# A two-layer trunk on one core: where the operands of the paired products are formed, and how many accumulators a pair unit has

## The chip, the cores and the metric

The kernel runs on one core of one Trainium2 chip. The metric is the device time of one launch in microseconds (us). TensorE (PE) multiplies, VectorE (DVE), ScalarE (ACT) and GpSimd (POOL) do elementwise work, and SyncE (SP), ACT and POOL issue transfers (DMA). Each engine works through its own queue in order and waits on semaphores for the others.

## The reference, cut to what matters

Two layers over 640 frames: 512 of a new stream and 8 x 16 of running streams, with 1024 channels. The first layer mixes by spatial gating and a gated convolution, the second by attention; after each mixer comes the same ConvFFN, and the change touches only that:

```python
def _conv_ffn(x, prev, w_up, conv_w, w_down):
    z, st = _causal_dwconv(x @ w_up, conv_w, prev)   # 1024 -> 2 * 2816, width 3
    gate, up = jnp.split(z, 2, axis=-1)
    return (jax.nn.silu(gate) * up) @ w_down, st     # 2816 -> 1024
```

`x` is RMS-normed before it enters; the outputs are the residual streams and the new states.

## The kernel before

**Precision.** A product in full precision is three PE passes: each operand is split into a high part (a cast by ACT, `hi`) and a low part (operand minus high part, by DVE, `lo`), and PE adds high x high, high x low and low x high. `part` (L133) does such a split; the program's names end in h and l (`hh`/`hl`, `sh`/`sl`, `whi`/`wlo`, `fbh`/`fbl`). `added` (L99) makes the low part another way: ACT writes minus the high part, and a transfer issued by POOL adds the source on top.

**Layout.** Channels lie on the 128 partitions, frames along the free side, in two halves of HT = 320. The 1024 input channels are 8 chunks `h[0..7]`, walked in the order `KORD` = 0, 2, 4, 6, 1, 3, 5, 7.

**The up-projection, 22 steps j for each layer, each with a gate block and an up block of 128 outputs.** Steps 0 to 3 are *full units*: 48 matmuls a block (8 chunks x 3 passes x 2 halves), and `pad_evac` (L329) multiplies the sums by `rb`, the inverse norm of each frame, on their way out of PSUM. Steps 4 to 21 are *pair units*: gate and up, the even and odd channel chunks and the two halves of the frames form a 2 x 2 product that is computed with seven products instead of eight (a Strassen-Winograd scheme). A product is 12 matmuls of 128 x 320 (four pairs of chunks x 3 passes). Their operands must be normed beforehand:

- `forms(p, ...)` (L145), for each of the four pairs p of chunks: DVE writes the normed chunks `y` (two operations over 640 frames), then their sums T1 to T4 (six operations over 320), T1 over a part of `y`, T2 to T4 into a `raw` buffer. The latter become `fbh`, `fbl` by `added`, with a transfer that reads the `raw` buffer. It is called after step 0 (p = 0, 1) and after step 1 (p = 2, 3), behind that step's convolution and gating (`act`, L489).
- `settle(p, h, form)` (L162): splits the eight `y` back into the tiles `hh`, `hl` of the chunks. These are the tiles that the full units read, so a chunk can be settled only when the last full unit has read it. The loop runs over p, so over the chunks 0, 1, 2, ... in the code.
- `pair_weights` (L171) loads a gate and an up block into two `raw` buffers, adds and subtracts in place on DVE (L180), and splits the seven weight operands. There are four `raw` buffers in all; full units, forms, pair units and down blocks share them.

**PSUM** has eight banks: two tiles `zx` of two banks, one tile `d` of two (down blocks and every third full unit), two tiles `aux` of one. A pair unit held two accumulators in the two halves of one `zx` tile, Z (the product y2a) and X (y1a, then T2, T1 and y2b added on), and a third, Y (T3, then T4), in an `aux` tile. Between the products `snap` (ACT, tiles `sn`) copies what has been summed so far: p1 after y1a, p7 after T3, u after T2; DVE makes the outputs `zg`, `zu` (tiles `zp`) of them.

**Down blocks.** Each pair unit carries two blocks of the down-projection of the part before it, each 24 matmuls into `d`, passed as `downs` and put between the products so that a snap has time. Their weights come by `weights_down` (L112): a load by SP, a cast by ACT (L120), its negative (L121), and a transfer by POOL (L122) that completes `wlo`.

**Order.** The code gives dependences and priorities; a scheduler settles the order on every engine when the program is built. Matmuls of different products, and of neighbouring units, are thus interleaved.

Of the kernel before, what the change touches and what calls it, by code (L numbers as in the profile page):

```python
# [8 lines left out]
F32 = mybir.dt.float32  # L9
# [3 lines left out]
ALU = mybir.AluOpType  # L13
# [3 lines left out]
P = 128  # L17
# [36 lines left out]
class Core:  # L54
# [106 lines left out]

    def settle(self, p, h, form):  # L162

        ys, fb = form
        for y, (hi, lo) in zip(ys, h):
            self.part(hi, lo, y)
        pick = lambda t, i: (t[0][:, i * HT:(i + 1) * HT], t[1][:, i * HT:(i + 1) * HT])
        return dict(y1a=pick(h[0], 0), t1=pick(h[0], 1), y2a=pick(h[1], 0), y2b=pick(h[1], 1),
                    t2=pick(fb, 0), t3=pick(fb, 1), t4=pick(fb, 2))

# [31 lines left out]

    def pair_blocks(self, w, f, zg, zu, states, downs):

        nc = self.nc
        zx = self.pz.tile([P, 1024], F32, tag="zx", name=self.nm("zx"))
        Z, X = zx[:, C0:512], zx[:, 512:512 + HT]
        Y = self.aux()[:, 0:HT]
        n = TP - HT
# [7 lines left out]
        for z, st in zip((zg, zu), states):  # L217
            nc.gpsimd.tensor_copy(out=str_(z)[:, :, 0:2], in_=st.rearrange("p (s c) -> p s c", c=2))
        self.product(X, w["x11"], f, "y1a", True)
        p1 = snap(X, 1.0)  # L220
        self.product(Z, w["x12"], f, "y2a", True)
        nc.vector.tensor_tensor(out=zg[:, 2:2 + HT], in0=Z, in1=p1, op=ALU.add)
        self.product(Y, w["s3"], f, "t3", True)
        p7 = snap(Y, -1.0)
        self.product(X, w["s2"], f, "t2", False)
        u = snap(X, -1.0)
        if downs:
            downs.pop(0)()
        self.product(X, w["s1"], f, "t1", False)
        nc.vector.tensor_tensor(out=zu[:, 2 + HT:514], in0=p7[:, 0:n], in1=X[:, 0:n], op=ALU.subtract)  # L230
        nc.vector.tensor_tensor(out=str_(zu)[:, :, 2:18], in0=v(p7), in1=v(X), op=ALU.subtract)
        self.product(Y, w["x22"], f, "t4", False)
        nc.vector.tensor_tensor(out=zu[:, 2:2 + HT], in0=u, in1=Y, op=ALU.subtract)
        if downs:
            downs.pop(0)()
# [248 lines left out]
    def ffn(self, l, x, h, g, rb, ring, fb, finish, out=None):  # L484
# [40 lines left out]
        for n, (a, b) in enumerate(PARTS):  # L525
# [4 lines left out]
            for j in range(a, b):  # L530
# [3 lines left out]
                if j < NSTD:  # L534
                    w = ahead.pop(0)
                    ps = self.blocks(w, hk, first) if j == 0 else [self.blocks([v], hk)[0] for v in w]
                    if j + 2 < NSTD:
                        ahead.append(full(j + 2))
                    elif j + 2 == NSTD:
                        ahead.append(part(j + 2))  # L540
                    else:
                        dn = downs(n, acts, 0)
                        f = [self.settle(p, (h[2 * p], h[2 * p + 1]), forms[p]) for p in range(4)]
                    for z, p_, st in zip((zg, zu), ps, sts):
                        self.pad_evac(z, p_[:, C0:C0 + T], rb, st)
                else:
                    if j == NSTD:
                        w = ahead.pop(0)
                        left.pop(0)
                    else:  # L550
                        w = part(j)
                        dn = downs(n - 1, prev, left.pop(0))
                    self.pair_blocks(w, f, zg, zu, sts, dn)
                for i, z in enumerate((zg, zu)):
                    self.new_state(z, so[:, i, 18 * (j - a):18 * (j - a) + 18])
                acts.append(act(zg, zu, j))
                if j < 2:
                    forms += [self.forms(p, x, g, rb, ring, fb) for p in (2 * j, 2 * j + 1)]
            nc.scalar.dma_start(out=two(io["o_sf"][l], NB)[:, :, 18 * a:18 * b], in_=so[:, :, 0:18 * (b - a)])
# [539 lines left out]
```

## Time and profile before

| | us |
|---|---|
| median of 3 runs | 1504.85 (1503.73 to 1508.41) |
| the profiled execution | 1505.12, with a span of 1503.3 |
| PE busy | 1464.5 (97% of the span) |
| DVE, ACT, POOL busy | 1042.1 (69%), 734.4 (49%), 200.7 (13%) |
| the ConvFFN of the first layer, first pair unit on PE | from 271.3 |
| the ConvFFN of the second layer, first pair unit on PE | from 1104.8 |

Rows of the timeline give start, duration, engine, line, operation, output<-inputs and shapes; the bracket gives how long the engine had been idle and who ended that. A row of waits gives total, times and longest. A row of windows gives for a stretch its length, then for each engine the busy time and instruction count, the granted PE clock, the DMA share and GB/s. Matmuls overlap: each lasts about 0.31 us and the next starts 0.147 us later.

### The profile page before, as it was taken

Reading aid. Unit: us, or ns where it says so; the run is one execution under the profiler, and the core shown is the slowest. Engines: PE = TensorE matmul, PEld = TensorE weight load, DVE = VectorE, ACT = ScalarE, POOL = GpSimd, SP = SyncE. Lnnn points to the kernel's source line nnn. Section 1 sums busy time; section 2 is a strip of 40 time slices with the busy share of each in tenths; the row PEclk is TensorE's granted clock in tenths of the full one; section 3 lists DMA queues with packets and bytes.
Section 4 is the critical chain, followed back from the end, with each engine's and each line's share of the span. In section 5 each row is a group of like instructions: output and inputs, shape, how many; then the busy total and the mean of one; then the engine's idle time right before and its main releaser. Section 6 shows DMA issues by size and latency. Waiting matters only on the chain.

```text
span 1503.3 us, 26371 instructions
## 1 busy us (share of the span) xinstructions
PE 1464.5 (97%) x10576; PEld 1412.7 (94%) x10576; DVE 1042.1 (69%) x1791; ACT 734.4 (49%) x1324; POOL 200.7 (13%) x237
## 2 busy tenths in 40 slices
PE   8999999899999999999999999999979999999998
PEld 6999999899999999999989888888979999999998
DVE  6555437976777778676676767768787768767764
ACT  5422325745555555445545454535565555545541
POOL 5100121300100010033111111003211010001000
PEclk9999999999999999999999999999999999999999
DMA  7222214634444434253534343422365434334432
GB/s 272 78 71 72 71 43 94 166 96 116 113 116 113 104 101 118 77 168 105 186 124 142 106 130 110 148 82 88 66 159 141 103 100 119 101 93 115 112 87 85
DMA packets 72938, 168.84 MB, mean 112 GB/s; under 512 B 13728, under 2 KB 21840, under 8 KB 72688
## 3 DMA queue, kind: packets, MB, share of 16 engines
q1 hardware_dynamic: 48304, 133.79, 27.9%
q0 software_dynamic: 11808, 25.96, 10.5%
q10 hardware_dynamic: 12704, 7.41, 1.6%
q8 instruction: 83, 1.36, 0.4%
q14 instruction: 39, 0.32, 0.1%
HBM read 147.43 MB, written 11.54 MB: 106 GB/s over the span
## 4 chain that ended last, share of the span: by engine, by line
PE 81%; DMA 7%; DVE 5%; ACT 4%; issue 2%; SPq 0%; ACTq 0%; POOL 0%; DVEq 0%; POOLq 0%
PE mm L250 33%; PE zx L200 16%; PE pj L701 12%; PE aux L200 7%; DMA wlo<-w_dn 5%; PE pv L777 3%; PE po L250 3%; PE pt L770 1%; DVE hl L281 1%; DVE wlo L95 1%; PE mm L388 1%; DMA fbl<-raw 1%; PE pt L856 1%; PE sc L763 1%; DVE t L347 1%
## 5 line engine op out<-in xcount | busy, mean ns | idle before, releaser
L135 ACT CAST sh<-raw 128x1024 fp32r<-128x1024 f32 (+1 forms) x144 | 135.1, 941 | 157.9 <-PE zx L200 93.7
L250 PE MATMUL mm<-sh,wlo 128*128 128x320 f32 x864 | 197.9, 310 | 8.3 <-DMA wlo<-w_dn 8.3
L250 PE MATMUL mm<-sh,whi 128*128 128x320 f32 x864 | 196.3, 309 | 1.5 <-ACT whi L120 0.8
L250 PE MATMUL mm<-sl,whi 128*128 128x320 f32 x864 | 196.7, 308 | 0.0
L136 DVE TENSOR_TENSOR sl<-raw,sh 128x1024 fp32r<-128x1024 f32 (+1 forms) x144 | 155.8, 1090 | 56.4 <-ACT sh L135 56.2
L200 PE MATMUL zx<-hh,sh 128*128 128x320 f32 x576 | 179.2, 311 | 8.4 <-ACT sn L215 8.3
L200 PE MATMUL zx<-hl,sh 128*128 128x320 f32 x576 | 178.8, 311 | 0.6 <-DVE hl L136 0.6
L200 PE MATMUL zx<-hh,sl 128*128 128x320 f32 x576 | 176.1, 311 | 0.7 <-DVE sl L136 0.7
L347 DVE SCALAR_TENSOR_TENSOR t<-zp,cst,t 128x656 f32<-128x656 f32 x184 | 164.2, 898 | 15.0 <-ACT t L345 13.3
L94 ACT CAST whi<-raw 128x1024 fp32r<-128x1024 f32 (+3 forms) x96 | 85.8, 895 | 145.1 <-PE mm L250 81.6
L250 PEld LDWEIGHTS mm<-sh,wlo 128*128 128x128 f32 x864 | 143.6, 188 | 12.0 <-DMA wlo<-w_dn 8.5
L358 DVE TENSOR_TENSOR x<-mm,x 128x640 f32<-128x640 f32 x103 | 84.6, 821 | 93.3 <-PE mm L250 93.2
L250 PEld LDWEIGHTS mm<-sh,whi 128*128 128x128 f32 x864 | 143.6, 188 | 2.9 <-ACT whi L120 1.3
L250 PEld LDWEIGHTS mm<-sl,whi 128*128 128x128 f32 x864 | 144.3, 188 | 0.2 <-DVE sl L136 0.2
L701 PE MATMUL pj<-whi,hl 128*128 128x256 f32 x480 | 137.9, 287 | 2.8 <-DVE hl L281 2.8
L701 PE MATMUL pj<-wlo,hh 128*128 128x256 f32 x480 | 137.6, 287 | 0.0
L701 PE MATMUL pj<-whi,hh 128*128 128x256 f32 x480 | 137.3, 287 | 0.0
L95 DVE TENSOR_TENSOR wlo<-raw,whi 128x1024 fp32r<-128x1024 f32 (+3 forms) x96 | 107.9, 1128 | 33.9 <-ACT whi L94 33.4
L250 PE MATMUL mm<-hl,whi 128*128 128x320 f32 x512 | 116.9, 309 | 2.0 <-DVE hl L281 2.0
L200 PEld LDWEIGHTS zx<-hh,sh 128*128 128x128 f32 x576 | 109.1, 189 | 9.2 <-ACT sn L215 8.9
L250 PE MATMUL mm<-hh,whi 128*128 128x320 f32 x512 | 117.1, 310 | 0.0
L250 PE MATMUL mm<-hh,wlo 128*128 128x320 f32 x512 | 116.5, 309 | 0.0
(235 smaller groups left out, 3353.0 us busy)
## 6 DMA issues: line engine op xcount, KB each, us to landing
raw<-w_up SPq DMA_DIRECT2D x88, 512.0 KB
raw<-w_dn SPq DMA_DIRECT2D x36, 512.0 KB
wlo<-w_dn POOLq DMA_DIRECT2D x36, 512.0 KB, 5.9
raw<-w_c SPq DMA_DIRECT2D x24, 512.0 KB
raw<-w_ab SPq DMA_DIRECT2D x16, 512.0 KB
ck<-c_k SPq DMA_DIRECT2D x16, 512.0 KB
cv<-c_v SPq DMA_DIRECT2D x16, 512.0 KB
o_kv<-z ACTq DMA_DIRECT2D x8, 640.0 KB
```

Source lines behind the costliest of these rows:

```text
L94: nc.scalar.copy(out=hi[:, c], in_=raw[:, c])
L95: nc.vector.tensor_tensor(out=lo[:, c], in0=raw[:, c], in1=hi[:, c].bitcast(F32), op=ALU.subtract)
L135: nc.scalar.copy(out=hi, in_=src)
L136: nc.vector.tensor_tensor(out=lo, in0=src, in1=hi.bitcast(F32), op=ALU.subtract)
L200: nc.tensor.matmul(out, lhsT=l[:, c], rhs=r, start=start and p == 0 and i == 0, stop=p == 3 and i == 2, skip_group_check=True)
L250: nc.tensor.matmul(outs[h], lhsT=l, rhs=r[:, h * HT:(h + 1) * HT], start=start and k == 0, stop=stop and k == 2)
L281: nc.vector.scalar_tensor_tensor(out=lo, in0=x, scalar=gs, in1=hi.bitcast(F32), op0=ALU.mult, op1=ALU.subtract)
L347: nc.vector.scalar_tensor_tensor(out=cv[:, 0:CW], in0=zp[:, i:i + CW], scalar=w[:, i:i + 1], in1=cv[:, 0:CW], op0=ALU.mult, op1=ALU.add)
L358: self.nc.vector.tensor_tensor(out=x, in0=ps[:, C0:C0 + T], in1=x, op=ALU.add)
L388: nc.tensor.matmul(pvs[tb], lhsT=l[:, tb * P:(tb + 1) * P], rhs=r[:, (kc % 2) * 512:(kc % 2 + 1) * 512], start=kc == 0 and k == 0, stop=kc ...
L701: nc.tensor.matmul(out[tb], lhsT=l[:, tb * P:(tb + 1) * P], rhs=r[:, c:c + 256], start=kc == 0 and i == 0, stop=kc == 7 and i == 2)
L777: nc.tensor.matmul(ov[64 * hh:64 * hh + 64, i * P:n], lhsT=z[2][:, j, (2 * pair + hh) * 64:(2 * pair + hh) * 64 + 64], rhs=u[:, j * P:(j + ...
```

## The change

Four edits:

1. `forms` for p = 0, 1 and p = 2, 3 is called right after the eviction of the gate block and of the up block of steps 0 and 1, instead of behind those steps' convolution and gating.
2. `settle` splits all eight chunks in one call in the order `KORD`, the order in which the last full unit leaves them.
3. A pair unit takes three tiles: X one bank of a `zx` tile, Y and Z both `aux` tiles. Both `aux` tiles are then held by one unit.
4. The products of a pair unit stand in another order: T3, y1a, T4, y2a, T2, T1, y2b (before: y1a, y2a, T3, T2, T1, T4, y2b), with the first down block between T2 and T1 and the second between T1 and y2b. In the first pair unit of a layer T3 and T4 come first, and both down blocks come at the end.

```diff
-    def settle(self, p, h, form):
-        ys, fb = form
-        for y, (hi, lo) in zip(ys, h):
-            self.part(hi, lo, y)
+    def settle(self, h, forms):
+        for c in KORD:
+            hi, lo = h[c]
+            self.part(hi, lo, forms[c // 2][0][c % 2])
...
-    def pair_blocks(self, w, f, zg, zu, states, downs):
-        zx = self.pz.tile([P, 1024], F32, tag="zx", name=self.nm("zx"))
-        Z, X = zx[:, C0:512], zx[:, 512:512 + HT]
-        Y = self.aux()[:, 0:HT]
+    def pair_blocks(self, w, f, zg, zu, states, downs, first=False):
+        X = self.pz.tile([P, 1024], F32, tag="zx", name=self.nm("zx"))[:, 0:HT]
+        Y, Z = self.aux()[:, 0:HT], self.aux()[:, 0:HT]
...
+        self.product(Y, w["s3"], f, "t3", True)
+        p7 = snap(Y, -1.0)
+        if first:
+            self.product(Y, w["x22"], f, "t4", False)
         self.product(X, w["x11"], f, "y1a", True)
         p1 = snap(X, 1.0)
+        if not first:
+            self.product(Y, w["x22"], f, "t4", False)
         self.product(Z, w["x12"], f, "y2a", True)
         nc.vector.tensor_tensor(out=zg[:, 2:2 + HT], in0=Z, in1=p1, op=ALU.add)
-        self.product(Y, w["s3"], f, "t3", True)
-        p7 = snap(Y, -1.0)
         self.product(X, w["s2"], f, "t2", False)
         u = snap(X, -1.0)
-        if downs:
+        nc.vector.tensor_tensor(out=zu[:, 2:2 + HT], in0=u, in1=Y, op=ALU.subtract)
+        if downs and not first:
             downs.pop(0)()
         self.product(X, w["s1"], f, "t1", False)
         nc.vector.tensor_tensor(out=zu[:, 2 + HT:514], in0=p7[:, 0:n], in1=X[:, 0:n], op=ALU.subtract)
         nc.vector.tensor_tensor(out=str_(zu)[:, :, 2:18], in0=v(p7), in1=v(X), op=ALU.subtract)
-        self.product(Y, w["x22"], f, "t4", False)
-        nc.vector.tensor_tensor(out=zu[:, 2:2 + HT], in0=u, in1=Y, op=ALU.subtract)
-        if downs:
+        if downs and not first:
             downs.pop(0)()
         self.product(X, w["s4"], f, "y2b", False)
...
-                        f = [self.settle(p, (h[2 * p], h[2 * p + 1]), forms[p]) for p in range(4)]
-                    for z, p_, st in zip((zg, zu), ps, sts):
+                        f = self.settle(h, forms)
+                    for i, (z, p_, st) in enumerate(zip((zg, zu), ps, sts)):
                         self.pad_evac(z, p_[:, C0:C0 + T], rb, st)
+                        if j < 2:
+                            forms.append(self.forms(2 * j + i, x, g, rb, ring, fb))
...
-                    self.pair_blocks(w, f, zg, zu, sts, dn)
+                    self.pair_blocks(w, f, zg, zu, sts, dn, j == NSTD)
...
-                if j < 2:
-                    forms += [self.forms(p, x, g, rb, ring, fb) for p in (2 * j, 2 * j + 1)]
```

The changed file has three more lines, so L250 of before is L253 of after, L339 is L342, L347 is L350, L497 is L500.

**DVE at step 0 of the first layer.** `zp_88`, `zp_89`, `zp_90` are the evictions, `t_2153`, `t_2177` and the like the convolutions, `y` the normed chunks, `raw_...<-y` the sums. Before, the first `y` stands behind the evictions and the convolution of step 0 and behind the eviction of the next block:

```order
L347 SCALAR_TENSOR_TENSOR t_2153<-zp_88,cst,t_2153 128x656
L347 SCALAR_TENSOR_TENSOR t_2149<-zp_89,cst,t_2149 128x656
L347 SCALAR_TENSOR_TENSOR t_2153<-zp_88,cst,t_2153 128x656
L339 TENSOR_TENSOR zp_90<-mm_2193,rb_1974 128x512
L340 TENSOR_TENSOR zp_90<-mm_2193,rb_1974 128x8x16
L500 TENSOR_TENSOR t_2158<-t_2153,t_2149 128x512
L501 TENSOR_TENSOR t_2158<-t_2153,t_2149 128x128
L152 SCALAR_TENSOR_TENSOR y_2165<-x_74,gv,rb_1974 128x640
```

Now the four `y` of this step stand ahead of its evictions (the rows before these), and the sums right behind them:

```order
L343 TENSOR_TENSOR zp_88<-mm_2030,rb_1974 128x8x16
L342 TENSOR_TENSOR zp_89<-mm_2031,rb_1974 128x512
L343 TENSOR_TENSOR zp_89<-mm_2031,rb_1974 128x8x16
L156 TENSOR_TENSOR raw_2148<-y_2145,y_2144 128x320
L156 TENSOR_TENSOR raw_2165<-y_2162,y_2161 128x320
L157 TENSOR_TENSOR y_2144<-y_2144 128x320
L157 TENSOR_TENSOR y_2161<-y_2161 128x320
L350 SCALAR_TENSOR_TENSOR t_2177<-zp_89,cst,t_2177 128x656
```

So the first sums moved ahead of the convolution that they stood behind.

**PE at the start of the first pair unit of the first layer.** `hh_1573`, `hh_1642`, `hh_1768`, `hh_1894` are the settled even chunks, `hh_1579` the first odd one. Before, the unit began with the twelve matmuls of y1a; its last even chunk is followed at once by y2a in the same tile `zx_2652`:

```order
L200 MATMUL zx_2652<-hh_1768,sl_2460 128x320
L200 MATMUL zx_2652<-hh_1894,sh_2459 128x320
L200 MATMUL zx_2652<-hl_1895,sh_2459 128x320
L200 MATMUL zx_2652<-hh_1894,sl_2460 128x320
L200 MATMUL zx_2652<-hh_1579,sh_2459 128x320
L200 MATMUL zx_2652<-hl_1580,sh_2459 128x320
```

Now it begins with T3 on the formed sums, in `aux_2653`:

```order
L253 MATMUL mm_2552<-hh_1957,wlo_2301 128x320 x2
L200 MATMUL aux_2653<-fbh_2153,sh_2469 128x320
L200 MATMUL aux_2653<-fbl_2154,sh_2469 128x320
L200 MATMUL zx_2652<-hh_1573,sh_2459 128x320
L200 MATMUL aux_2653<-fbh_2153,sl_2470 128x320
L200 MATMUL aux_2653<-fbh_2170,sh_2469 128x320
```

T3 moved ahead of y1a; T4 and the first matmuls of a down block follow, ahead of all but one matmul of y2a.

**PE at T2 and T1 of the same unit.** Before, T4 (in `aux_2653`, with `sh_2463`) stood behind T2, and the next unit's matmuls between T4 and T1:

```order
L200 MATMUL zx_2652<-fbh_2352,sh_2475 128x320
L200 MATMUL zx_2652<-fbl_2353,sh_2475 128x320
L200 MATMUL zx_2652<-fbh_2352,sl_2476 128x320
L200 MATMUL aux_2653<-fbh_2174,sh_2463 128x320
L200 MATMUL aux_2653<-fbl_2175,sh_2463 128x320
```

Now T1 (with `sh_2469`) follows T2 with nothing in between, both in `zx_2652`:

```order
L200 MATMUL zx_2652<-fbh_2334,sh_2475 128x320
L200 MATMUL zx_2652<-fbl_2335,sh_2475 128x320
L200 MATMUL zx_2652<-fbh_2334,sl_2476 128x320
L200 MATMUL zx_2652<-hh_1573,sh_2469 128x320
L200 MATMUL zx_2652<-hl_1574,sh_2469 128x320
```

The work that stood between T2 and T1 moved ahead of T2.

More of the change, by code (lines that the diff above doesn't have):

```diff
@@ L160, in forms @@
         return ys, self.added(fb, ("fbh", "fbl"), t, t, 3 * HT, 3 * HT)
-    def settle(self, p, h, form):
-        ys, fb = form
-        for y, (hi, lo) in zip(ys, h):
-            self.part(hi, lo, y)
+    def settle(self, h, forms):
+        for c in KORD:
+            hi, lo = h[c]
+            self.part(hi, lo, forms[c // 2][0][c % 2])
         pick = lambda t, i: (t[0][:, i * HT:(i + 1) * HT], t[1][:, i * HT:(i + 1) * HT])
-        return dict(y1a=pick(h[0], 0), t1=pick(h[0], 1), y2a=pick(h[1], 0), y2b=pick(h[1], 1),
-                    t2=pick(fb, 0), t3=pick(fb, 1), t4=pick(fb, 2))
+        return [dict(y1a=pick(h[2 * p], 0), t1=pick(h[2 * p], 1), y2a=pick(h[2 * p + 1], 0), y2b=pick(h[2 * p + 1], 1),
+                     t2=pick(fb, 0), t3=pick(fb, 1), t4=pick(fb, 2)) for p, (_, fb) in enumerate(forms)]
     def pair_weights(self, gate, up):
```

## The prediction, on record before the result

> **What bounds the kernel now.** I read the page first, then PE's waits, then stretches of the span, then the places with waits row by row.
>
> ```profile
> span 1503.3 us, 26371 instructions
> PE 1464.5 (97%) x10576; PEld 1412.7 (94%) x10576; DVE 1042.1 (69%) x1791; ACT 734.4 (49%) x1324; POOL 200.7 (13%) x237
> PE zx L200 <- ACT sn L215: 8.3, 2, 4.6
> PE mm L250 <- DMA wlo<-w_dn: 8.3, 11, 1.6
> ```
>
> PE is the bound; nothing makes this kernel faster that doesn't take PE's idle or slow time away, 39 us at most as idle (1503.3 less 1464.5). The largest waits of the pair units are two for a snap, one in each layer, in the first pair unit. The windows around it, from the last full unit's end to the first matmul of y2b, and the steady pair units behind:
>
> ```profile
> 227.60:271.10 43.50, 43.50 (x298) 43.50 (x298) 34.77 (x60) 23.56 (x35) 8.33 (x14) 1.00 0.45 99
> 271.10:298.72 27.62, 22.03 (x126) 20.40 (x124) 26.33 (x40) 22.29 (x33) 10.47 (x6) 0.88 0.70 176
> 300.00:640.00 340.00, 336.75 (x2290) 335.27 (x2289) 248.32 (x358) 175.75 (x292) 30.26 (x49) 1.00 0.43 106
> 1063.10:1104.70 41.60, 41.60 (x286) 41.60 (x285) 35.29 (x61) 22.07 (x34) 6.42 (x10) 1.00 0.44 96
> 1104.70:1134.32 29.62, 21.38 (x124) 19.62 (x123) 26.17 (x39) 21.98 (x33) 3.54 (x6) 0.88 0.68 173
> 1145.00:1480.00 335.00, 330.55 (x2245) 328.88 (x2244) 242.10 (x348) 171.65 (x283) 27.90 (x47) 1.00 0.41 103
> 303.86 3.52 PE mm L250 x24
> ```
>
> The last row (the chain) gives the full pace, 3.52 / 24 = 0.147 us a matmul. In the second and fifth window 122 matmuls stand in the program's order up to y2b; at full pace they take 17.9 us. They took 27.6 and 29.6: **9.7 and 11.7 us are lost, 21.4 together**. In the steady windows PE is idle for 3.3 of 340 and 4.5 of 335 us. In the lost stretches DVE is full (26.3 of 27.6); ahead of them, while PE runs its full units unbroken, DVE is idle for 8.7 of 43.5 and 6.3 of 41.6 us. Row by row, PE first:
>
> ```profile
> 273.78 0.31 PE L200 MATMUL zx<-hh,sl 128*128 128x320 f32 x1
> 277.83 0.63 PE L200 MATMUL zx<-hh,sh 128*128 128x320 f32 x1 [3.74 <-ACT sn L215]
> 278.26 0.47 PE L200 MATMUL zx<-hl,sh 128*128 128x320 f32 x1
> 278.53 0.47 PE L200 MATMUL zx<-hh,sl 128*128 128x320 f32 x1
> 282.81 0.43 PE L200 MATMUL aux<-fbh,sh 128*128 128x320 f32 x1
> 284.52 0.42 PE L200 MATMUL zx<-fbh,sh 128*128 128x320 f32 x1 [0.55 <-ACT sh L135]
> 1106.37 0.31 PE L200 MATMUL zx<-hh,sl 128*128 128x320 f32 x1
> 1111.27 0.64 PE L200 MATMUL zx<-hh,sh 128*128 128x320 f32 x1 [4.59 <-ACT sn L215]
> 1116.40 0.41 PE L200 MATMUL aux<-fbh,sl 128*128 128x320 f32 x1 [1.03 <-DVE sl L136]
> 1116.65 0.30 PE L200 MATMUL aux<-fbh,sh 128*128 128x320 f32 x1
> 1116.80 0.31 PE L200 MATMUL aux<-fbl,sh 128*128 128x320 f32 x1
> ```
>
> y1a ends, y2a waits 3.7 and 4.6 us, and behind that pause a matmul starts every 0.27 us for some 5 us before it is 0.147 again. Why the wait is that long, from ACT, then DVE's settling:
>
> ```profile
> 273.32 0.72 ACT L135 CAST hh<-y 128x640 fp32r<-128x640 f32 x1
> 276.11 1.33 ACT L135 CAST hh<-y 128x640 fp32r<-128x640 f32 x2
> 277.36 0.42 ACT L215 ACTIVATE sn<-zx 128x320 f32<-128x320 f32 x1
> 1110.80 0.42 ACT L215 ACTIVATE sn<-zx 128x320 f32<-128x320 f32 x1
> 277.13 1.55 DVE L136 TENSOR_TENSOR hl<-y,hh 128x640 fp32r<-128x640 f32 x2
> ```
>
> The first odd chunk's high part was there at 274.0, yet y2a started when the snap p1 was done (277.78). y1a and y2a share one `zx` tile, so y2a waits for the snap that reads y1a, and the snap stands on ACT behind the last cast of the settling. Without that wait PE would still have met the low parts of the odd chunks, the last of which DVE had at 278.7, 4.9 us after y1a's end.
>
> **The change part by part.** Arithmetic is the same: 12 matmuls a product, three snaps, the same forms, splits and transfers. What moves:
>
> *Separate tiles.* y2a no longer waits for the snap of y1a. That takes away the wait named above, but only as far as chunks and weights are there.
>
> *T3 and T4 first.* They need `fb` tiles and weights, not the settled chunks. Now 12 matmuls of T3, 12 of y1a, 4 of a down block and 12 of T4 are ahead of the odd chunks: 40 x 0.147 = 5.9 us, before 1.8 (y1a alone).
>
> *Forms between evictions.* They must be ready for T3 to go first. Before and now:
>
> ```profile
> 227.35 0.27 ACT L325 COPY rb<-aux 128x128 f32<-128x128 f32 x1
> 237.88 1.68 DVE L152 SCALAR_TENSOR_TENSOR y<-x,gv,rb 128x640 f32<-128x640 f32 x2
> 253.89 1.68 DVE L152 SCALAR_TENSOR_TENSOR y<-x,gv,rb 128x640 f32<-128x640 f32 x2
> 256.74 0.89 POOL L104 DMA_DIRECT2D fbl<-raw  x1 [3.08 <-issue]
> 264.15 0.33 SPq L177 DMA_DIRECT2D raw<-w_up  x1
> 275.29 0.87 POOL L104 DMA_DIRECT2D fbl<-raw  x1 [0.75 <-ACT fbl L103]
> 280.98 0.34 SPq L176 DMA_DIRECT2D raw<-w_up  x1
> DMA to landing us min/median/max: 4.5/6.7/8.2
> ```
>
> `rb` is there at 227.6; the first `y` can go then, not at 237.9. Walking the new DVE order with these durations (a `y` 0.8 us from start to start, sums 0.4, evictions 0.8) the second forms begin near 245 instead of 253.9 and their transfers near 265 instead of 273.7 and 275.3; the load of the first pair unit's weights, which waits for a `raw` buffer to be read out by the transfer before (256.74 to 264.15), moves from 264 to about 251. The four `y` cost the first eviction 3.2 us of delay; its tile is needed again two blocks of 7.0 us later, so this is hidden by PE's own matmuls. POOL's queue gets the copies of states ahead of the later transfers; they are short and wait for convolutions, which the same walk has done before 265. SP's order is the same. DVE gains at most its idle time, 8.7 and 6.3 us; a loss of 9.7 and 11.7 us, during which it was full, can therefore shrink mostly but not vanish, and less in the second layer.
>
> *Settling in KORD order.* Same instructions; each chunk's split no longer queues behind one that is released later.
>
> *What takes the place, in the first pair units.* (a) First layer: T1 directly behind T2, so PE waits for the snap u. (b) Second layer: y2b directly behind T1, so PE waits for two DVE subtractions. Their prices:
>
> ```profile
> L215 ACT ACTIVATE sn<-zx x72: 423/438/451, 277.4 to 1458.7; 128x320 f32<-128x320 f32 x72
> PE zx L200: 52.8, 37
> 291.09 0.48 DVE L233 TENSOR_TENSOR zp<-sn,aux 128x320 f32<-128x320 f32 x1
> 1129.62 0.35 DVE L230 TENSOR_TENSOR zp<-sn,zx 128x192 f32<-128x192 f32 x1
> 1129.88 0.28 DVE L231 TENSOR_TENSOR zp<-sn,zx 128x128 f32<-128x128 f32 x1
> ```
>
> (a) 0.44 and the signals, 0.6; up to 1.6 with a cast of 1.05 ahead of it. (b) 0.54 and the signals, 0.7; up to 1.9. (c) DVE's settling in the second layer: in my walk eight low parts, 0.75 us each, begin there 2.6 us behind PE's last full unit and set the pace of y1a and y2a for a while (DVE stands some 5 us there, from 1088 to 1093, for the first pair unit's load, since `rb` comes 2 us later against PE than in the first layer): 2.0, between 0 (as in the first layer) and 4.6 (as now). (d) Loads: the next unit's weights still wait for the second forms' transfers to land (4.5 to 8.2 us); ACT's queue holds p7 and p1 behind the cast of that load. 1.0 in the first layer and 1.5 in the second, between 0 and 4 each. (e) The first down block's `wlo`: 0.8, its longest wait so far being 1.6. (f) The last `fbl` for T3: 0.3 each. (g) In the second pair unit T4 stands six matmuls (0.88 us) behind T3, against 0.44 for p7: 0.4 each, none if ACT is free. Sum: 0.6 + 0.7 + 2.0 + 2.5 + 0.8 + 0.6 + 0.8 = **8.0**, between 1.3 ((a), (b)) and about 16.
>
> *Steady pair units.* Each snap keeps at least 23 matmuls (3.4 us) between product and use in the new order, as before. New is that Y of the next unit may need the bank that this unit's subtraction releases. The trace has no such wait; bounds are nothing and 1.0 us at each of 34 boundaries (snap 0.44, subtraction 0.48, signals). Nearest is nothing, as the snap's own row shows that ACT was idle for PE at 37 of its turns; I take 1.3 in all, also for down blocks' waits that fall differently.
>
> Sum against the profiled execution (1505.12, 0.3 above the median): 21.4 less 8.0 less 1.3 is 12.1 saved, so 1493.0.
>
> **The rivals.** *The stall only moves.* T3 first, but weights and chunks late as now: DVE does the same work, and if its idle time isn't used (its waits for ACT between forms and convolutions are still there), PE waits a few us inside T3 and y1a. For it: DVE full at 26.3 of 27.6. Against: the forms stand 9 to 10 us earlier in DVE's queue. Price: of 21.4 all but 3 lost again, 1502.
>
> *A broken-up unit at half clock.* PE's many short waits in the first pair unit keep the slow pace. From the rows, 282.81 less 278.26 are 17 matmuls at 0.27, 2.1 us lost; that in each layer again, beside the waits above, is 4.2: 1497.2. Against it: behind the wait of 1.03 us, at 1116.40, the pace was 0.15 again from the second matmul on (1116.65 to 1116.80). [...]
>
> *Slower: the Y bank.* Both `aux` tiles are held by one unit; if the next T3 waits for this unit's subtraction, PE loses up to 1.0 us at 34 boundaries: 1493 + 34 = 1527. It decides from 12.1 / 34 = 0.36 us each. For it: in some places of the new order T3 begins two matmuls behind T2. Against: there the other bank, Z, is long free, and the program may take that.
>
> **How the numbers follow.** The sum as worked out 0.62, half clock 0.12, the stall moves 0.15, the Y bank 0.11. 0.3% of 1505, 4.5 us, is about what a measurement can tell from no change. Faster takes the first two, 0.74; same, the third and a mild Y bank, 0.16; slower 0.10. The range goes from 21.4 less 1.3 (20.1 saved, 1485; I take 1486) to the stall that only moves (1503), and leaves out the Y bank.
>
> **What would show it.** Right: in the first pair unit no PE wait above 2 us, none for a snap of y1a; the first pair units' loss 3 us and 5 us by the same count; the granted clock at 1.0 there; loads of the first pair weights 8 us or more earlier; steady windows with 3 to 6 us idle. Wrong: waits for DVE's `hl` of more than 4 us in the second layer; PE waits for `zp` subtractions at unit boundaries; more waits for `wlo<-w_dn` than 8.3 us.

## The result, and the profile after

| | before | changed |
|---|---|---|
| median of the runs, us | 1505.75 (1503.73 to 1508.41, 4 runs) | 1485.68 (1485.11 to 1487.40, 4 runs) |
| ratio, 95% interval | | 0.9873 (0.9857 to 0.9890) |
| the profiled execution, span, us | 1505.12, 1503.3 | 1485.11, 1483.3 |

The change saves 20 us, 1.3%. Forecast were 12.1 us and 1493.0, in a range from 1486 to 1503: the sign was right, the size too small, and the median lies 0.3 us below the low end. In the table of the experiments the ratios leave out four executions that ran slow as a whole (e2 2015 us, e8 1759, e5 1568 and 1572); the medians are over all. From the page of the changed kernel, and its list of PE's waits (total, times, longest):

```profile
span 1483.3 us, 26325 instructions
PE 1459.0 (98%) x10576; PEld 1409.5 (95%) x10576; DVE 1038.1 (70%) x1791; ACT 734.5 (50%) x1324; POOL 207.4 (14%) x237
...
PE mm L253 <- DMA wlo<-w_dn: 3.0, 3, 1.1
PE aux L200 <- ACT sn L214: 1.2, 2, 0.9
PE zx L200 <- ACT sh L135: 0.9, 1, 0.9
PE zx L200 <- DVE zp L236: 0.6, 1, 0.6
...
PE zx L200 <- ACT sn L214: 0.5, 1, 0.5
```

The two waits of 3.7 and 4.6 us for a snap are gone, and of 8.3 us for `wlo` 3.0 are left. The windows of the first pair units (to the first matmul of y2b) and of the later units:

```profile
272.82:290.59 17.77, 16.03 (x104) 14.98 (x103) 17.01 (x28) 11.53 (x19) 2.91 (x3) 1.00 0.70 191
300.00:638.00 338.00, 338.00 (x2309) 337.99 (x2308) 248.20 (x362) 176.02 (x290) 29.72 (x48) 1.00 0.43 106
...
1094.88:1113.88 19.00, 16.19 (x105) 14.88 (x103) 16.00 (x27) 12.38 (x21) 5.78 (x4) 1.00 0.50 144
1130.00:1463.00 333.00, 330.95 (x2255) 330.26 (x2254) 240.58 (x348) 172.03 (x284) 29.13 (x47) 1.00 0.42 103
```

The program now has 102 matmuls ahead of y2b in each first pair unit, 15.0 us at the full pace of 0.147. They took 17.77 and 19.00: **2.8 and 4.0 us are lost, where it was 9.7 and 11.7**. The granted clock stays at 1.00, where it was 0.88. In the steady window of the first layer PE has no idle time at all; in the second, 2.0 us.

So that whole kernels can be compared, the table below gives for every run the *pair stretch* of each layer, from the first matmul of its first pair unit to the first matmul behind the pair units (the attention's first, the last projection's first). Before they are 390.9 and 389.1 us, after 379.6 and 378.9: 11.3 and 10.1 less. Of that 6.9 and 7.7 lie in the first pair unit, the other 4.4 and 2.4 behind it. Against these 21.4 us (a sum of its own, not the prediction's 21.4 us of loss) stand 1.5 us by which the first pair unit of the changed execution began later (272.82 for 271.27); that comes from the start of the program, which the change doesn't touch, and which varies as much in the runs below (271.3 to 273.1, but for e7).

### The profile page after: what moved, and what is told of

Same layout as the page of the kernel before. It is cut to its first block, busy times and chain, and to the rows that moved or that the text cites. A ratio compares the mean times of both kernels' runs of the same rounds, so it can differ in the third digit from the quotient of the medians.

```text
span 1483.3 us, 26325 instructions
## 1 busy us (share of the span) xinstructions
PE 1459.0 (98%) x10576; PEld 1409.5 (95%) x10576; DVE 1038.1 (70%) x1791; ACT 734.5 (50%) x1324; POOL 207.4 (14%) x237
## 4 chain that ended last, share of the span: by engine, by line
PE 88%; DVE 4%; ACT 3%; DMA 3%; issue 1%; SPq 0%; ACTq 0%; DVEq 0%
PE mm L253 35%; PE zx L200 16%; PE pj L704 12%; PE aux L200 12%; PE pv L780 3%; PE po L253 3%; PE pt L773 1%; DMA wlo<-w_dn 1%; DVE hl L284 1%; PE mm L391 1%; DVE wlo L95 1%; PE pt L859 1%; PE sc L766 1%; DMA raw<-w_dn 1%; ACT sh L135 1%
## 5 line engine op out<-in xcount | busy, mean ns | idle before, releaser
L253 PE MATMUL mm<-sh,wlo 128*128 128x320 f32 x864 | 197.0, 309 | 3.0 <-DMA wlo<-w_dn 3.0
L253 PE MATMUL mm<-sh,whi 128*128 128x320 f32 x864 | 196.6, 309 | 0.6 <-ACT sh L135 0.5
L253 PE MATMUL mm<-sl,whi 128*128 128x320 f32 x864 | 196.6, 308 | 0.0
L350 DVE SCALAR_TENSOR_TENSOR t<-zp,cst,t 128x656 f32<-128x656 f32 x184 | 164.5, 897 | 37.2 <-ACT t L348 35.8
L253 PEld LDWEIGHTS mm<-sh,wlo 128*128 128x128 f32 x864 | 144.0, 188 | 4.2 <-DMA wlo<-w_dn 4.2
L253 PEld LDWEIGHTS mm<-sh,whi 128*128 128x128 f32 x864 | 143.8, 188 | 1.7 <-ACT sh L135 1.0
L253 PEld LDWEIGHTS mm<-sl,whi 128*128 128x128 f32 x864 | 144.3, 188 | 0.2 <-DVE sl L136 0.2
L200 PE MATMUL zx<-hh,sh 128*128 128x320 f32 x432 | 133.6, 309 | 2.1 <-ACT sh L135 0.9
L200 PE MATMUL zx<-hl,sh 128*128 128x320 f32 x432 | 133.1, 308 | 0.0
L200 PE MATMUL zx<-hh,sl 128*128 128x320 f32 x432 | 131.0, 308 | 0.0
L253 PE MATMUL mm<-hl,whi 128*128 128x320 f32 x512 | 116.9, 309 | 2.0 <-DVE hl L284 2.0
L253 PE MATMUL mm<-hh,whi 128*128 128x320 f32 x512 | 117.1, 310 | 0.0
L253 PE MATMUL mm<-hh,wlo 128*128 128x320 f32 x512 | 116.5, 309 | 0.0
L704 PEld LDWEIGHTS pj<-whi,hl 128*128 128x128 f32 x480 | 91.6, 191 | 4.6 <-DVE hl L284 3.5
```

What stands on the lines that cost most here:

```text
L200: nc.tensor.matmul(out, lhsT=l[:, c], rhs=r, start=start and p == 0 and i == 0, stop=p == 3 and i == 2, skip_group_check=True)
L253: nc.tensor.matmul(outs[h], lhsT=l, rhs=r[:, h * HT:(h + 1) * HT], start=start and k == 0, stop=stop and k == 2)
L350: nc.vector.scalar_tensor_tensor(out=cv[:, 0:CW], in0=zp[:, i:i + CW], scalar=w[:, i:i + 1], in1=cv[:, 0:CW], op0=ALU.mult, op1=ALU.add)
L704: nc.tensor.matmul(out[tb], lhsT=l[:, tb * P:(tb + 1) * P], rhs=r[:, c:c + 256], start=kc == 0 and i == 0, stop=kc == 7 and i == 2)
```

## The experiments

Each ratio is to the kernel before as it ran beside that run (medians 1505.7 to 1506.9). The last two columns split what a pair stretch loses against a matmul every 0.1466 us (the 376.5 us of e7's first layer, for 2568 matmuls): in its first 150 matmuls, which take in the first pair unit whatever its order, and in the 2418 and 2382 behind them. They come from the starts of the matmuls in the profiled execution; first layer, second layer.

| run | edits | median, us | ratio to before, 95% | pair stretches, us | waits for `wlo<-w_dn`, us | lost in the first 150, us | lost behind them, us |
|---|---|---|---|---|---|---|---|
| before | none | 1505.75 | | 390.9, 389.1 | 8.3 | 9.6, 11.7 | 4.8, 6.2 |
| changed | all | 1485.68 | 0.9857 to 0.9890 | 379.6, 378.9 | 3.0 | 3.1, 5.0 | 0, 2.8 |
| e1 | 3 | 1498.61 | 0.9938 to 0.9973 | 386.5, 385.1 | 1.3 | 9.8, 13.0 | 0.3, 0.9 |
| e2 | 1, 2 | 1495.75 | 0.9910 to 0.9951 | 385.1, 383.6 | 5.7 | 7.8, 7.2 | 0.8, 5.2 |
| e3 | 1, 2, 3 | 1488.62 | 0.9862 to 0.9905 | 379.9, 381.6 | 4.3 | 3.1, 8.4 | 0.4, 2.0 |
| e4 | 2, 3, 4 | 1500.98 | 0.9959 to 0.9986 | 388.4, 386.3 | 4.2 | 11.9, 13.5 | 0.1, 1.7 |
| e5 | 1, 2, 4 | 1556.43 | 1.0267 to 1.0332 | 423.1, 421.9 | 54.7 | 7.8, 7.0 | 38.8, 43.7 |
| e6 | 3, 4 in later units | 1508.29 | 1.0004 to 1.0024 | 393.4, 387.2 | 7.6 | 10.2, 15.9 | 6.7, 0.1 |
| e7 | all, forms in step 0 | 1514.96 | 1.0041 to 1.0066 | 376.5, 372.8 | 1.2 | 0, 0 | 0, 1.6 |
| e8 | all (the changed kernel) | 1487.19 | 0.9853 to 0.9887 | 379.6, 378.2 | 2.6 | 3.0, 4.4 | 0.2, 2.5 |
| e9 | all, low parts by DVE | 1483.78 | 0.9838 to 0.9871 | 378.1, 378.8 | none | 1.7, 7.5 | 0, 0 |
| e10 | 1, 2, 4, low parts by DVE | 1486.47 | 0.9858 to 0.9891 | 380.4, 380.0 | none | 2.9, 7.7 | 1.0, 1.2 |
| e11 | all, forms behind the gate | 1485.56 | 0.9852 to 0.9895 | 379.5, 379.7 | 3.1 | 3.0, 5.5 | 0.1, 3.0 |
| e12 | all, three forms in step 0 | 1493.93 | 0.9907 to 0.9942 | 381.7, 386.3 | 4.4 | 5.2, 13.0 | 0.1, 2.1 |

Three parts of the change needed no run. Written with the chunks settled in the order 0, 1, 2, ..., or without the case `first`, or with the first down block kept in the first pair unit, the program that the scheduler makes has on all five engines the same instructions in the same order (a few buffer numbers differ). So edit 2 and the special case of the first pair unit do nothing here: the scheduler takes what is ready. What can count is edit 1, edit 3 and the order T3, y1a, T4 in the code.

**e1, three tiles alone.**

```diff
-        zx = self.pz.tile([P, 1024], F32, tag="zx", name=self.nm("zx"))
-        Z, X = zx[:, C0:512], zx[:, 512:512 + HT]
-        Y = self.aux()[:, 0:HT]
+        X = self.pz.tile([P, 1024], F32, tag="zx", name=self.nm("zx"))[:, 0:HT]
+        Y, Z = self.aux()[:, 0:HT], self.aux()[:, 0:HT]
```

> The kernel before with edit 3 alone: X in a zx tile, Y and Z in aux tiles; forms, settling and the order of products in the code as before. In the program's order the closest down block now stands 45 matmuls behind the y2b of the unit before it, where it stood 17 to 21 five times in each layer. Theory 1 (two gains: early forms fill the first pair unit, and separate tiles take the snap out of y2a's way and keep the down blocks away from the unit before): the waits for wlo fall from 8.3 to 3 us or less, and of the first pair units' loss of 21.4 us only the part goes that was the snap alone, 1 to 3 us a layer, since the odd chunks' low parts are late as before; 1495 to 1499 us. Theory 2 (early forms are the whole gain, and the fewer waits for wlo come with them): 1503 to 1506 us, waits for wlo at 8 us. Theory 3 (the shared tile was the whole stall): 1489 us or less.

1498.6, as theory 1 had it. In its timeline of PE (first layer) the wait for the snap is gone, and the next ones show themselves:

```profile
274.73 0.41 PE L200 MATMUL aux<-hh,sh 128*128 128x320 f32 x1 [1.80 <-ACT hh L135]
277.12 0.42 PE L200 MATMUL aux<-hl,sh 128*128 128x320 f32 x1 [0.44 <-DVE hl L136]
280.36 0.41 PE L200 MATMUL aux<-fbh,sh 128*128 128x320 f32 x1 [2.42 <-ACT sh L135]
```

y2a (now in `aux`) waits for the settled chunk, then T3 for the weights' cast. The snap was the last of three late things, and with it gone the next two take its place: the first 150 matmuls lose 9.8 and 13.0 us, no less than before. That each layer is still some 4 us shorter comes from the later units, where the waits for `wlo` are nearly gone. Theory 1 had the time right and expected 1 to 3 us a layer from the first pair units, which did not come.

**e2, early forms alone**: the changed kernel with the pair unit of before.

> The changed kernel with the pair unit of before (edits 1 and 2 without 3 and 4: Z and X share one zx tile). In the program's order T3 and y1a fill the first 24 matmuls of the first pair unit, y2a stands 6 behind, and the closest down blocks stand 17 to 22 matmuls behind the y2b before them, as in the kernel before. Theory 1: the first pair units lose 3 to 5 us each instead of 9.7 and 11.7 (early forms, with a short wait for the snap of y1a, 0.5 to 1.5 us), the steady units keep their waits for wlo, 7 to 8 us; 1492 to 1495 us. Theory 2: as the changed kernel, 1485 to 1487 us, waits for wlo at 3 us. Theory 3: y2a still waits 3 to 4 us in each layer for its snap; 1500 us or more.

1495.75, 0.75 above theory 1's range. The wait for the snap fell to 0.7 us in one layer and to none in the other, though X and Z share their tile: the work that the early forms bring lies between y1a and y2a. 2.3 and 2.2 us for weights (`sh`) are left in the first pair units, and 2.5 for `wlo` in one: the first 150 matmuls lose 7.8 and 7.2 us where theory 1 had 3 to 5, and 4 us of the gain lie in the first layer's later units, where it had none.

**e3, both, with the products in the old order.**

> The changed kernel without edit 4: three tiles, early forms, KORD settling, but the products in the code's old order (y1a, y2a, T3, T2, T1, T4, y2b, a down block behind T2 and one behind T4). T3 then stands on PE at matmuls 11 to 23 and 6 to 18 of the first pair unit anyway. Theory 1: the order of the products in the code matters little, since the program takes what is ready; within 2 us of the changed kernel, 1485 to 1488 us; one down block in the second layer stands 19 matmuls behind a y2b and waits about 1.5 us. Rival: T3 and T4 ahead of everything are worth the rest, 3 us a layer: 1491 us or more.

1488.6: 17.1 us less than before, and e1 and e2 alone give 7.1 and 10.0, so by medians the two add up. Against the changed kernel 1.4 to 2.9 us are missing (1487.2, 1485.7), between the two cases that were expected. The intervals overlap: that edit 4 is worth something there is likely, and no more can be said.

**e4, late forms with tiles and order new.**

> The changed kernel without edit 1: the forms stand behind each step's convolution and gating, as before; three tiles, KORD settling and the new order of products are kept. In the program's order y1a comes first again, and 48 matmuls at least lie between a y2b and the next down block. Theory 1: waits for wlo at 3 us or less (5 us less than before), the first pair units still late, with DVE full there: 7 us lost a layer instead of 9.7 and 11.7; 1493 to 1497 us. Theory 2 (early forms are the whole gain): 1503 to 1506 us. Theory 3 (the tiles are the whole gain): 1485 to 1488 us.

1501.0 lies between the ranges of theories 1 and 2: all three were off. The first 150 matmuls lose 11.9 and 13.5 us, more than before; what e4 gains lies in the later units, as in e1. Without early forms the new order loses 2.4 us against e1, by medians. Two rows of its PE waits:

```profile
PE aux L200 <- ACT sh L135: 12.5, 2, 7.3
...
PE mm L253 <- DMA wlo<-w_dn: 4.2, 3, 1.7
```

T3 stands early in the program and waits 5.2 and 7.3 us for the split weights. In the first layer their second load starts at 264.65 us (251.09 in the changed kernel), behind the late forms, and is in by 268.2; the sums and the cast of T3's weights then stand between the settling of the chunks, on DVE until 276.4 and on ACT at 278.97. T3 first pays only where edit 1 lets the load go early.

**e5, early forms and new order, one shared tile.**

```diff
+        zx = self.pz.tile([P, 1024], F32, tag="zx", name=self.nm("zx"))
+        Z, X = zx[:, C0:512], zx[:, 512:512 + HT]
+        Y = self.aux()[:, 0:HT]
```

> The changed kernel with X and Z back in the two halves of one zx tile (edits 1, 2 and 4 without 3). In the program's order 18 matmuls lie between y1a and y2a of the first pair unit, enough for the snap, and the closest down blocks stand 14 to 16 matmuls behind a y2b, five times in each layer, where the changed kernel has 46. Theory 1 (separate tiles are worth the steady units' waits and a part of the first unit; the runs so far give 7 us for them at early forms and the old order of products): 1490 to 1494 us, waits for wlo at 6 us or more. Theory 2 (the order of products makes up for the tile): 1485 to 1488 us, waits for wlo at 3 us.

1556: slower than any of the kernels, by a mechanism that none of my theories had at this size. (Its executions spread from 1543 to 1572; the profiled one is the longest, and the four shortest have a median of 1553.) From its waits, and from the rows of the transfers of the down weights' low parts in the kernel before, e1 and e5, in this order:

```profile
PE mm L254 <- DMA wlo<-w_dn: 54.7, 26, 3.8
```

```profile
DMA to landing us min/median/max: 5.7/5.9/8.1
```

```profile
DMA to landing us min/median/max: 5.7/5.8/6.2
```

```profile
DMA to landing us min/median/max: 5.7/6.7/8.8
```

One such wait of e5, from ACT, SP, POOL and PE:

```profile
514.61 1.05 ACT L120 CAST whi<-raw 128x1024 fp32r<-128x1024 f32 x1 [1.47 <-PE mm L254]
513.58 0.38 SPq L119 DMA_DIRECT2D raw<-w_dn  x1
515.68 0.33 SPq L176 DMA_DIRECT2D raw<-w_up  x1
517.17 1.22 POOL L122 DMA_DIRECT2D wlo<-w_dn  x1 [1.55 <-ACT wlo L121]
525.42 0.56 PE L254 MATMUL mm<-sh,wlo 128*128 128x320 f32 x2 [2.95 <-DMA wlo<-w_dn]
```

A down block ends and releases the buffer; the cast starts at once, the transfer 2.56 us later (514.61 to 517.17), and lands 5.7 to 8.8 us behind that. With the 5.9 us of before's median that is 8.5 us, 58 matmuls. In the program's order more than half of the down tiles of before, e1 and the changed kernel stand 58 to 65 matmuls behind the down block ahead of them: just enough, with little to spare. In e5 half stand 52 or 53 behind, 7.6 us; its few tiles at 58 waited nowhere (0.06 us at most), nearly all the others did. In these rows late landings stand beside loads issued shortly before: in e5, where half of the landings took 6.7 us or more, the load of the next down weights stands mostly 3.6 us ahead of the transfer (513.58), as it does for before's three waits of 1.5 to 1.6 us, whose transfers landed after 7.9 to 8.1 us; in before all seven landings of more than 7 us have that load 3.3 to 3.7 us ahead. In e1 it stands 5.7 us ahead or is far, and its latest landing took 6.2 us. That is a coincidence seen in many rows, no proof: two transfers of the changed kernel landed after 7.1 and 7.7 us with that load 5.2 and 4.9 us ahead.

**e6, tiles and new order in the later units only.**

> The kernel before with edits 3 and 4 in the second and later pair units only; forms, settling and the first pair unit as before. The closest down blocks stand 46 matmuls behind a y2b. Theory 1: the first pair units keep their loss (waits for the snap of y1a of 3 to 5 us), the later units' waits of 7.7 us for wlo fall to 2.5 us or less; 1499 to 1502 us. Theory 2 (the later units wait less only because the first units leave them in another phase): 1504 to 1506 us, 6 us or more of waits for wlo.

1508.3: theory 1 fell, it still waits 7.6 us for `wlo`. 2.3 of them are in the second layer's first pair unit, the other 5.3 at four places, one in each part of the first layer. One of these, from ACT, POOL and PE:

```profile
381.17 1.05 ACT L120 CAST whi<-raw 128x1024 fp32r<-128x1024 f32 x1 [2.31 <-PE zx L200]
382.12 0.31 ACT L280 COPY zp<-zx 128x192 f32<-128x192 f32 x1
382.33 0.27 ACT L281 COPY zp<-zx 128x128 f32<-128x128 f32 x1
382.49 1.06 ACT L135 CAST sh<-raw 128x1024 fp32r<-128x1024 f32 x1
383.43 1.07 ACT L121 ACTIVATE wlo<-whi 128x1024 fp32r<-128x1024 f32 x1
384.92 1.21 POOL L122 DMA_DIRECT2D wlo<-w_dn  x1 [3.78 <-ACT wlo L121]
390.80 0.53 PE L293 MATMUL mm<-sh,wlo 128*128 128x320 f32 x2 [1.33 <-DMA wlo<-w_dn]
```

Here y2b releases the buffer (`PE zx L200`), and with it two copies and a weight cast come between the cast and the negative on ACT: 3.75 us to the transfer instead of 2.56, and 5.9 more to land, 9.7 us. These tiles stand 56 to 58 matmuls behind y2b, 8.2 to 8.5 us, so PE waits 1.33 us; in the second layer they stand 65 to 67 behind and don't wait. So the distance counts, but the 46 that I had taken for enough from the changed kernel are enough only where y2b is not the releaser. What e6 gains in the second layer (387.2 for 389.1) it loses in the first (393.4 for 390.9). In the second layer's later units next to nothing is lost (0.1 us, before 6.2), but its first pair unit loses 4.2 more, with that wait of 2.3.

**e7, all forms in step 0.**

```diff
-                        if j < 2:
-                            forms.append(self.forms(2 * j + i, x, g, rb, ring, fb))
+                        if j == 0:
+                            forms += [self.forms(p, x, g, rb, ring, fb) for p in (2 * i, 2 * i + 1)]
```

> The changed kernel with all four pairs formed in step 0, two behind each eviction, instead of in steps 0 and 1. In the program's order the first pair unit then reads T3, y1a, T4 and y2a nearly unbroken. Theory 1 (what is left of the first pair units' loss, 2.5 to 3 us each, is lateness of forms and chunks): 1482 to 1485 us. Rival: four forms hold all four raw buffers, the weights of full units 2 and 3 come late, and PE waits there for whi or wlo; 1488 us or more.

1515.0, the rival. Its waits:

```profile
PE mm L253 <- ACT whi L102: 19.2, 4, 6.5
PE mm L253 <- DMA wlo<-w_up: 11.0, 2, 6.2
```

The pair stretches are the shortest of all (376.5 and 372.8), yet some 37 us are lost ahead of them, 30.2 of it in these waits, in full units 2 and 3, whose weights need the `raw` buffers that the forms hold. The first 150 matmuls lose nothing. How much of that is the earlier forms can't be told, since a pause of some 18 us ahead of each layer's pair units also gave everything else time to be ready.

**e8, the changed kernel again.**

> The changed kernel itself, on the same chip as the other three, for comparison: 1485 to 1488 us, with the waits of its first profile: no wait above 1.2 us from the first pair units on but for DVE's hl between the layers' parts.

1487.2, the same waits.

**e9 and e10, the down weights' low parts by DVE**, in the changed kernel and in e5:

```diff
-        nc.scalar.copy(out=hi[:, 0:m], in_=raw[:, 0:m])
-        nc.scalar.mul(out=lo[:, 0:m], in_=hi[:, 0:m].bitcast(F32), mul=-1.0)
-        nc.gpsimd.dma_start(out=two(lo), in_=src, accum_op=ALU.add)
+        self.part(hi[:, 0:m], lo[:, 0:m], raw[:, 0:m])
```

> The changed kernel with the low parts of the down weights made by a DVE subtraction (1.2 us each, 36 of them) instead of ACT's negative and a transfer: no wlo<-w_dn transfer is left. Theory 1 (the later units wait for wlo when that transfer lands 7 us or more after its issue instead of 5.9): no wait of PE for the down weights' low parts is left in the later units, 2 to 3 us less; 1482 to 1486 us. Rival: DVE, busy 248 of 338 us in a steady stretch and 25 us more now, is late for snaps' sums or weights, and PE waits for it; 1488 us or more.

> The slow combination (shared zx tile with early forms and the new order of products, 1556 us), with the down weights' low parts made by DVE, so without the transfers. Theory 1 (its 54.7 us of waits for wlo are transfers that land 7 to 9 us after their issue, where 52 matmuls, 7.6 us, lie between the release of the buffer and the use): the waits go, 1495 to 1505 us. Rival (the shared tile itself holds PE back, and the waits are put down to the transfer because it comes last): 1540 us or more, with PE waiting for zx, sn or zp instead.

e10 decides it: 1556.4 became 1486.5 with the shared tile kept, so the chain of negative and transfer was the cause, and the tile itself costs little (2.7 us against e9 by medians, with intervals that overlap). The two profiled executions are 84.8 us apart (1571.9 and 1487.1), not only the 54.7 of listed waits: the mean granted clock over the span rose from 0.982 to 0.998, some 25 us of 1570, so the pace behind those waits had been slow too, which the expectation's 1495 had left out. e9 is at 1483.8 the fastest kernel of this study. The windows of its later units:

```profile
300.00:638.00 338.00, 338.00 (x2309) 338.00 (x2308) 270.51 (x380) 162.55 (x276) 9.61 (x31) 1.00 0.27 82
1130.00:1463.00 333.00, 333.00 (x2274) 332.99 (x2273) 265.40 (x371) 158.99 (x270) 6.53 (x31) 1.00 0.27 79
```

PE has no idle time in either, with DVE at 270.5 of 338 us (248.2 in the changed kernel) and the DMA share at 0.27 instead of 0.43. One new wait takes some of it back, in the first pair unit of the second layer:

```profile
1103.32 0.41 PE L198 MATMUL aux<-fbh,sh 128*128 128x320 f32 x1 [3.58 <-ACT sn L212]
```

Against the changed kernel it gains 2 to 3 us; the two intervals overlap (0.9838 to 0.9871 and 0.9853 to 0.9890), so that this version beats the kernel before is measured, that it beats the changed one is likely only.

**e11 and e12, forms a block earlier, or three in step 0.**

> The changed kernel with both pairs of a step formed behind the gate block's eviction, so pairs 1 and 3 one block of 7 us earlier. Theory 1 (what the first pair units still lose, 2.5 to 3 us each, is lateness of forms and weights): 1 to 3 us less, 1483 to 1485 us. Rival: the second eviction comes later by two forms, 5 us, PE's next block in that PSUM tile waits, or the raw buffers are taken from the full units' weights; 1488 us or more.

> The changed kernel with three pairs formed in step 0 and the fourth behind the gate block's eviction of step 1. With four in step 0 PE waited 30 us for weights of full units 2 and 3 (whi 19.2, wlo<-w_up 11.0), while the pair stretches took 3 and 6 us less. Theory 1 (each raw buffer that a form holds in step 0 delays one load of a full unit): with three, the waits for whi and wlo<-w_up in the full units fall to some 10 to 20 us in all; 1492 to 1505 us. Rival (one free buffer is enough): none of those waits, 1480 to 1484 us.

e11 is the same as the changed kernel (1485.6): neither theory. e12 at 1493.9 lies in theory 1's range, but not for its reason: its list of waits has none for `whi` or `wlo` of a full unit; the pair stretches, above all the second (386.3), are longer, with waits of 1.4 to 2.8 us for `hl`, `sh` and `wlo`; in the second, behind waits of 1.44 (1097.54) and 0.72 us (1100.68), matmuls start mostly 0.27 us apart from 1101.12 to 1104.59. Why a third form in step 0 makes the second layer's first pair unit late was not followed further.

## Why the prediction was right or wrong, point by point

*What bounds, and separate tiles: the wait was right, the worth of the tiles lay elsewhere.* The two waits for the snap were what stood last (e1: gone with the tile split alone), and what came next were late chunks and weights, as written. These took the whole gain: with the tiles alone the first 150 matmuls lose 22.8 us in the two layers, before 21.3. What the tiles bring alone they bring in the later units (1.2 us lost there, before 11.0), where the prediction had expected nothing of them.

*Early forms: right.* A window of the changed kernel, and rows of its DVE, SP and POOL:

```profile
229.10:272.60 43.50, 43.50 (x299) 43.50 (x298) 39.93 (x68) 30.88 (x44) 13.75 (x16) 1.00 0.57 118
...
229.20 3.27 DVE L152 SCALAR_TENSOR_TENSOR y<-x,gv,rb 128x640 f32<-128x640 f32 x4 [4.01 <-ACT rb L328]
246.36 1.67 DVE L152 SCALAR_TENSOR_TENSOR y<-x,gv,rb 128x640 f32<-128x640 f32 x2
...
248.76 0.33 SPq L176 DMA_DIRECT2D raw<-w_up  x1
251.09 0.33 SPq L177 DMA_DIRECT2D raw<-w_up  x1
...
266.92 1.77 POOL L104 DMA_DIRECT2D fbl<-raw  x2 [0.66 <-issue]
```

The second forms begin at 246.4 (walked: 245), their transfers at 266.9 (265), the weights' second load at 251.1 (251; before 264.15). DVE's idle time in the last 43.5 us before the unit went from 8.7 to 3.6 (43.50 less 39.93). That the loss can "shrink mostly but not vanish, and less in the second layer": 2.8 and 4.0.

*The terms of what takes the place: 8.0 forecast, 6.8 measured.* PE's waits in the two units:

```profile
275.31 0.42 PE L200 MATMUL aux<-fbl,sh 128*128 128x320 f32 x1 [0.27 <-DMA fbl<-raw]
284.04 0.42 PE L200 MATMUL zx<-hh,sh 128*128 128x320 f32 x1 [0.53 <-ACT sn L214]
288.43 0.56 PE L253 MATMUL mm<-sh,wlo 128*128 128x320 f32 x2 [0.91 <-DMA wlo<-w_dn]
1097.44 0.42 PE L200 MATMUL aux<-hh,sh 128*128 128x320 f32 x1 [0.35 <-ACT hh L135]
1101.23 0.41 PE L200 MATMUL zx<-hh,sh 128*128 128x320 f32 x1 [0.87 <-ACT sh L135]
1102.71 0.41 PE L200 MATMUL aux<-fbh,sh 128*128 128x320 f32 x1 [0.92 <-ACT sn L214]
1113.88 0.41 PE L200 MATMUL zx<-hh,sh 128*128 128x320 f32 x1 [0.65 <-DVE zp L236]
```

(a) the snap u, 0.6: 0.53. (b) the two subtractions, 0.7: 0.65. (d) in the second layer, 1.5: 0.87 for weights and 0.92 for a snap; in the first, 1.0: none. (e) 0.8: 0.91. (f) 0.3: 0.27, in one layer. (g) 0.4 each: 0.3 in one. (c), DVE's settling in the second layer, 2.0: one wait of 0.35 for a high part, none for a low part. Settling began at 1094.89 with PE's first pair matmul (1094.88), not 2.6 us behind it as walked, and T3 and the down block ahead of the chunks covered it: 0, the low end, was right. The seven rows make 4.5. The other 2.3 of 6.8 stand around them: from the matmul ahead of a wait to the second one behind it the starts show some 0.27 us more than the bracket (283.20 to 284.29 around the snap u: 1.09 for 0.53 and two steps of 0.147), and two stops too short for a bracket, both at the first matmul of a down block (277.22 and 1104.76), cost 0.3 each. (g) lies in the second pair unit; the first 150 matmuls, which take it in, lose 3.1 and 5.0, against 3 and 5 forecast. That the sum fits better than its parts is luck: with (g) the rows make 4.8 of 8.0, (c) being the furthest off, and what the terms had not counted, the 0.27 at each wait and the short stops, makes up for it with 3.3.

*KORD settling, and T3 and T4 first in the first pair unit: no effect of their own.* The programs with and without them, that is without the order `KORD` in `settle` or without the case `first`, are the same. I had listed the first as a help and had taken the second from the code; the programs built with each edit undone would have shown it beforehand.

*Steady pair units: this term failed.* It stood at a cost of 1.3 us, and the pair stretches behind the first unit gained 6.8 (4.4 and 2.4). The waits for `wlo` there, 7.7 us before, went to 2.0. This is nearly all that the forecast missed: the first units gave 14.6 for 13.4, this term 6.8 for -1.3, and the late start took 1.5. PE's idle time in the steady windows, named as a sign at 3 to 6 us, was 0 and 2.0. That the saving nearly met the low end of the range (20.1) is a coincidence, since that end stood for first pair units that lose nothing. I had bounded only what the change could add (the Y bank, other places of down blocks) and not what the trace showed to be there already, a wait that a new order can take away; "below nothing too" was left out. The runs show what hangs on it: transfers that have about 58 matmuls to land in, and land in time or not by the order (e1 none late in the later units, e5 54.7 us, e6 7.6). The rows of before did not tell on which side the changed order would fall; that it could fall on either, they did, and the distances could have been counted in the two orders. Between e5 and e1 the same term moved by over 50 us, so the slower side was open more than my 0.10 said, though by this path and not by the Y bank, of which no run shows a wait.

*The rivals.* The stall that only moves did not come here, but it did in e1 and e4, where the forms are late: 22.8 and 25.4 us lost in the first 150 matmuls, in e4 with 12.5 us of waits for `sh`. The broken-up unit at half clock did not come: waits of 0.27 to 0.92 us in a row, and the granted clock at 1.00 and the pace at 0.147 us throughout.

## What to carry to other kernels

Where a transfer's way from the release of its buffer to its first reader is as long as the matmuls that the order puts between (8.5 us against 58 matmuls here), any change of order is also a draw on those transfers: list the existing waits for them as a gain or a loss before costing the edit itself. Edits that make work available and edits that make a consumer early need each other: early forms were worth 10 us alone and the separate tiles 7, but none of those 7 where the tiles were meant to help, as long as the forms were late. T3 first cost 2 us without early forms; the 1.4 to 2.9 us that it brings with them are likely, not shown clear of the spread. Before costing an edit of code order under a scheduler, look whether the built program differs at all.

## What the runs showed of the hardware

In the changed kernel's first pair units PE waited 0.92 us at most and the granted clock stayed at 1.00; of two waits above 2 us in e2, one was followed by a slower pace and the other not. Mean over the first 28 us from the first pair matmul, changed kernel (both layers), then e2 (both layers), whose longest waits in the first layer are 2.48 and 2.30 us:

```profile
272.82:300.82 28.00, 26.25 (x172) 24.91 (x171) 25.18 (x38) 18.57 (x31) 5.22 (x6) 1.00 0.62 178
1094.88:1122.88 28.00, 24.90 (x160) 23.07 (x159) 25.00 (x39) 20.90 (x35) 7.21 (x6) 1.00 0.47 137
```

```profile
271.25:299.25 28.00, 22.80 (x140) 21.74 (x139) 21.44 (x33) 15.03 (x24) 1.84 (x3) 0.94 0.53 143
1100.34:1128.34 28.00, 24.60 (x144) 23.38 (x143) 23.18 (x37) 17.92 (x29) 5.80 (x4) 0.88 0.45 130
```

Rows of PE in e2's first layer, around these two waits:

```profile
278.77 0.41 PE L200 MATMUL zx<-hh,sh 128*128 128x320 f32 x1 [2.30 <-ACT sh L135]
...
279.49 0.31 PE L200 MATMUL zx<-hh,sl 128*128 128x320 f32 x1
279.64 0.31 PE L200 MATMUL zx<-hh,sh 128*128 128x320 f32 x1
...
286.82 0.53 PE L250 MATMUL mm<-sh,wlo 128*128 128x320 f32 x2 [2.48 <-DMA wlo<-w_dn]
...
289.91 0.47 PE L200 MATMUL zx<-fbh,sh 128*128 128x320 f32 x1
290.18 0.47 PE L200 MATMUL zx<-fbl,sh 128*128 128x320 f32 x1
290.44 0.47 PE L200 MATMUL zx<-fbh,sl 128*128 128x320 f32 x1
```

Behind the wait of 2.30 us the matmuls start 0.147 us apart (279.49 to 279.64), behind that of 2.48 us 0.27 apart (289.91 to 290.18) and 0.147 again from 291.21. The mean of 0.94 over 28 us makes some 1.7 us (0.06 x 28), an estimate of what the slower pace cost there beside the wait itself. Why one of two waits so close in length was followed by it and the other not was not shown: no run moved such a wait by itself.
